# Two early loads of a convolution kernel moved from SyncE's queue to ScalarE's

## The chip, the cores and the metric

The kernel runs on one core of a Trainium2 chip. Times are microseconds on the device for one execution of the whole kernel; the lower the better. The time before is the median of three runs, 104.27 us (104.04 to 104.47).

## The reference

The reference is a 3x3 convolution with zero padding, stride 1 and no bias, followed by a 2x2 maximum pool. It takes 16 images of 64 channels and 64x64 pixels and gives 128 channels of 32x32, all in 32-bit floats:

```python
x_pad = np.pad(x, ((0, 0), (0, 0), (pad, pad), (pad, pad)))
conv[b, co] += weight[co, ci, kh, kw] * x_pad[b, ci, kh:kh+h, kw:kw+w]   # over ci, kh, kw
output[b, c, i, j] = np.max(conv[b, c, 2*i:2*i+2, 2*j:2*j+2])
```

## The kernel before

**Tiling.** Two images lie on the 128 partitions together, 64 channels each. A pair of images is cut into four chunks of 16 rows, and a chunk gives 8 pooled rows. There are 8 pairs, so 32 chunks, numbered 0 to 31 in the order in which they are worked. For each chunk and each of its two images (`l` = 0 or 1) TensorE makes products of 64 input channels against 128 output channels with up to 512 columns; the two images use the upper and the lower 64 rows of the array, so their products run in pairs. All arithmetic of TensorE is in bfloat16, its sums stand in eight PSUM banks.

**Two kinds of chunk.** Of the two rows that are pooled together, the kernel does not compute each with three row taps. It forms sums and differences of weights, and for some chunks of input rows too, so that a pair of rows needs fewer products. `SEQ` says which form a chunk takes. A `K` chunk (0, 2, 5, 9, 14, 18, 23, 27) needs five products, `PAa`, `PAb`, `PBa`, `PBb`, `PR`, and reads the input as bfloat16 rows, tile `kx`. A `W` chunk (all others, the first is 1) needs four products, `P2`, `P0`, `P3`, `P1`, and reads sums and differences of neighbouring rows, tiles `we`, `ws` and `wv`, which VectorE or GpSimd make from 32-bit input rows, tile `wx`.

**The order is written out by hand.** `ORDER` is a list of tokens; the loop at line 513 takes them one by one and emits the instructions of each. Every engine works its own instructions in the order in which the tokens name them, and waits on semaphores for what it needs. The letter after a colon names the engine of a step (`v` VectorE, `a` ScalarE, `g` GpSimd), or a digit names a PSUM bank. What is needed here:

- `LW` loads the weights into `wraw` (line 533). `LX.s` loads chunk `s` as 32-bit floats: a `W` chunk into `wx` (line 262), a `K` chunk into `kf` (line 268). `LX.0a` and `LX.0b` are the two halves of chunk 0. `LX.2` and `LX.4`, `LX.8`, `LX.6`, `LX.7`, `LX.10`, `LX.11` follow. All of these are issued by SyncE and stand in one DMA queue. Later K chunks are loaded by GpSimd with a cast on the way (`LK`, line 272). `ST` stores a finished chunk, mostly through SyncE's queue, the last ones partly through ScalarE's (line 495).
- `c.m` forms the weight block `m` (lines 191, 196), `T.m` transposes it on TensorE (line 229), `TV.m` copies it out of PSUM into `wt` (lines 240 to 244).
- `E.s`, `S.s`, `V.s` make the differences and sums of a W chunk (line 196, tiles `we`, `ws`, `wv`). With `CP.s` ScalarE first copies one row set into PSUM (line 287), and VectorE's `E` and `S` read it from there (line 291).
- `XO` and `XE` cast the odd or even rows of a K chunk from `kf` to `kx` (lines 191, 193).
- `EV` copies a finished sum out of PSUM (lines 420, 422), `SE` copies a sum from one bank into another as the start of the next one, a seed (line 436), `MX` takes the maximum over two rows (line 440), `OD` and `CM` that over two columns (lines 463, 472).

**The start.** The first tokens load the weights, then chunk 1 (`LX.1`), then the two halves of chunk 0, then chunk 3, and interleave this with forming the weights. On VectorE the steps are, in order: `c.GS`, `c.D0`, `c.GM`, `c.D2`, then `E.1`, `c.GP`, `V.1`, `TV.GP`, `XO.0a`. On ScalarE: `c.g1`, `c.g0`, `c.g2`, four `TV`, the seeds `SE.1.0` and `SE.1.1`, `XO.0b`, `XE.0a`, `CP.3`. On TensorE: eight products that only set the banks (line 500), the transposes, `P2.1` for both images, two more sets of transposes with one product of the tile `zeros` between them (line 430), then `P0.1`, `PAa.0` (upper half), `P3.1`, and from there on without end. The `zeros` product sets a PSUM bank that has held transposed weights to a defined state. The tile `zeros` is filled by VectorE with a memset, line 169.

**Semaphores of the queue.** SyncE's and ScalarE's loads and stores use eight semaphores in turn, so that the ninth is issued only once the first has landed.

Of the kernel before, what the change touches and what calls it, by code (L numbers as in the profile page):

```python
# [13 lines left out]
SEQ = "KWKWWKWWWKWWWWKWWWKWWWWKWWWKWWWW"  # L14
ADDED = ()
ORDER = """
LW c.g1:a c.GS:v c.D0:v LX.1 c.GM:v c.D2:v LX.0a c.g0:a T.G0:0 T.GM:1 T.G1:2 E.1:v c.g2:a T.D2:3
TV.GM:a TV.G0:a T.G2:4 TV.D2:a LX.0b LX.3 P2.1.0:5 P2.1.1:6 TV.G2:a c.GP:v SE.1.0:7 V.1:v T.D0:1
LX.2 SE.1.1:0 T.GP:3 LX.4 TV.GP:v XO.0b:a XO.0a:v P0.1.1 P0.1.0 PAa.0.0a:4 PAa.0.1a:3 S.1:g P3.1.0
P3.1.1 TV.D0:v LX.8 XE.0a:a CP.3:1 PAa.0.1b PAb.0.0a TV.G1:v E.3:v S.3:v EV.1.1 EV.1.0 XE.0b:a  # L20
PAa.0.0b PAb.0.1a MX.1.1 PBa.0.1a:2 PBa.0.0a:6 PAb.0.0b PAb.0.1b V.3:g PBb.0.0a PBb.0.1a LX.6 XE.2:a
# [62 lines left out]
def kernel(  # L84
# [7 lines left out]
    nc = tc.nc  # L92
    FP32 = mybir.dt.float32
    BF16 = mybir.dt.bfloat16
# [13 lines left out]
    const = ctx.enter_context(tc.tile_pool(name="const", bufs=1))  # L108
# [16 lines left out]
    def behind(inst, other):  # L125
        if other is not None:
            tc.add_manual_dep(inst.ins, other.ins.name, SYNC, reason="order")
# [7 lines left out]
    def rows_of(p, lo, hi):  # L135
        return x[2 * p : 2 * p + 2].rearrange("b c h w -> (b c) h w")[:, lo:hi, :]

    def chunk(s):

        p, q = place[s]  # L140
        same = any(place[t] == (p, q - 1) and SEQ[t] == SEQ[s] for t in range(N))
        lo = 2 * R * q + 1 if same else max(0, 2 * R * q - 1)
        return p, lo, min(H, 2 * R * (q + 1) + 1)

    def half(s):
        return 2 * R * place[s][1] + R + 1
# [18 lines left out]
    wq = const.tile([CO, 7, 2, 2, CI], BF16)  # L165
    wt = const.tile([128, 7 * K, CO], BF16)
    gsum = const.tile([CO, 3, CI], FP32)
    zeros = const.tile([128, 512], BF16)
    nc.vector.memset(zeros, 0.0)
    ident = const.tile([128, 128], BF16)  # L170
    make_identity(nc, ident)
    wv = wraw.rearrange("a (c k) -> a k c", k=K * K)

    def ring(t, k):
# [69 lines left out]
            nc.vector.tensor_copy(out=dst, in_=src)  # L244


    kf = {}
    done = {}
    AHEAD = {"W": 12, "K": 13}

    def paced(s, inst):

        for l in (0, 1):
            behind(inst, done.get((s - AHEAD[SEQ[s]], l)))
        if SEQ[s] == "K" and s < AHEAD["K"] and s not in kf:
            behind(inst, done["head"])

    def load(s, part, e):
        p, lo, hi = chunk(s)
        if SEQ[s] == "W":  # L260
            t = wx[p % NWX]
            paced(s, nc.sync.dma_start(out=t[:, lo + 1 : hi + 1, :], in_=rows_of(p, lo, hi)))
            return
        if s not in kf:
            kf[s] = const.tile([128, hi - lo, W], FP32, name=f"kf_{s}")
        a, b = {"": (lo, hi), "a": (lo, half(s)), "b": (half(s), hi)}[part]
        q = nc.scalar if e == "a" else nc.sync
        paced(s, q.dma_start(out=kf[s][:, a - lo : b - lo, :], in_=rows_of(p, a, b)))

    def load_cast(s):  # L270
# [242 lines left out]
    for token in ORDER.split():  # L513
        what, _, at = token.partition(":")
        name, *args = what.split(".")
        if name in PRODUCTS:
            s, l = int(args[0]), int(args[1][0])
# [20 lines left out]
        elif name == "LX":  # L538
            load(int(args[0].rstrip("ab")), args[0].lstrip("0123456789"), at)
        elif name == "LK":  # L540
            load_cast(int(args[0]))
        elif name == "CP":
            lift(int(args[0]), int(at))
        elif name in ("XO", "XE"):
            to_bf16(int(args[0].rstrip("ab")), args[0].lstrip("0123456789"), int(name == "XO"), at)
        elif name in ("KS", "S", "E", "V"):
            f = rs_cast if name == "S" and int(args[0]) in ADDED else None
            (f or {"KS": ks, "S": rs, "E": re, "V": rv}[name])(int(args[0]), at)
        elif name in ("Ve", "Vo"):
            rv_half(int(args[0]), at, int(name == "Vo"))  # L550
        elif name == "SA":
            rs_add(int(args[0]))
        elif name == "ST":
            l, part = (int(args[1][0]), args[1][1:]) if len(args) > 1 else (None, "")
            store(int(args[0]), l, part, at)
        else:
            s = int(args[0])
            l, part = (int(args[1][0]), args[1][1:]) if len(args) > 1 else (None, "")
            if name in ("SE", "SEv"):
                bank["B", s, l] = int(at)  # L560
                seed(s, l, name[2:])
                continue
            if name in ("OD", "CM", "RM"):
                {"OD": odd, "CM": colmax, "RM": pairmax}[name](s, l, part)
            else:
                {"EV": evac, "MX": rowmax}[name](s, l)
# [36 lines left out]
```

## Time and profile before

| What | Value |
|---|---|
| Median of three runs | 104.27 us |
| The profiled execution | 103.89 us |
| Its span, first to last instruction | 102.1 us |
| TensorE busy | 95.6 us, 94% |
| VectorE busy | 90.0 us, 88% |
| ScalarE busy | 89.6 us, 88% |
| GpSimd busy | 80.8 us, 79% |
| TensorE's granted clock | 1.0 of full speed throughout |
| Read from HBM, written | 17.07 MB, 8.39 MB |
| SyncE's queue (q1) | 12,624 packets, 22.16 MB |
| ScalarE's queue (q10) | 288 packets, 0.20 MB |

The profile is one execution, taken by the hardware profiler; its engines are PE (TensorE), PEld (TensorE's weight loads), DVE (VectorE), ACT (ScalarE), POOL (GpSimd) and SP (SyncE). An engine's name with a small q (SPq, ACTq) stands for the part that issues DMAs and waits on semaphores. In a row of the timeline stand the start, the duration, the engine, the line and the operation, what is written and read, the number of instructions merged, and in brackets how long the engine was idle before and what ended that. In a row of the DMA issues the last number is the time from issue to landing. The chain is followed back from the last instruction: at each step to what released it.

### The profile page before, as it was taken

Reading aid. Unit: us, or ns where it says so; the run is one execution under the profiler, and the core shown is the slowest. Engines: PE = TensorE matmul, PEld = TensorE weight load, DVE = VectorE, ACT = ScalarE, POOL = GpSimd, SP = SyncE. Lnnn points to the kernel's source line nnn. Section 1 sums busy time; section 2 is a strip of 40 time slices with the busy share of each in tenths; the row PEclk is TensorE's granted clock in tenths of the full one; section 3 lists DMA queues with packets and bytes.
Section 4 is the critical chain, followed back from the end, with each engine's and each line's share of the span. In section 5 each row is a group of like instructions: output and inputs, shape, how many; then the busy total and the mean of one; then the engine's idle time right before and its main releaser. Section 6 shows DMA issues by size and latency. Waiting matters only on the chain.

```text
span 102.1 us, 2481 instructions
## 1 busy us (share of the span) xinstructions
PE 95.6 (94%) x870; PEld 52.3 (51%) x870; DVE 90.0 (88%) x176; ACT 89.6 (88%) x200; POOL 80.8 (79%) x63
## 2 busy tenths in 40 slices
PE   6698999999999999999999999999999999999940
PEld 2155954555555567565555575555444446455310
DVE  1596999999989999999999999778989999998780
ACT  5597999888999999998899999999998988999930
POOL 5005998999599969999998999999971999999000
PEclk9999999999999999999999999999999999999999
DMA  2989999849940699999999971898769955302353
GB/s 42 343 235 414 418 419 335 181 113 356 263 122 0 165 219 324 250 322 328 255 404 350 377 287 28 251 251 219 282 213 311 340 179 180 128 32 74 132 182 103
DMA packets 13789, 24.07 MB, mean 236 GB/s; under 512 B 1104, under 2 KB 9680, under 8 KB 13776
## 3 DMA queue, kind: packets, MB, share of 16 engines
q1 hardware_dynamic: 12624, 22.16, 64.8%
q0 software_dynamic: 864, 1.56, 8.8%
q10 hardware_dynamic: 288, 0.20, 0.6%
q8 instruction: 7, 0.11, 0.4%
q14 instruction: 6, 0.05, 0.1%
HBM read 17.07 MB, written 8.39 MB: 249 GB/s over the span
## 4 chain that ended last, share of the span: by engine, by line
PE 84%; DVE 6%; DMA 3%; ACT 3%; issue 1%; ACTq 0%; DVEq 0%
PE acc L405 84%; DMA wraw<-in_weight_dram 3%; DVE wq L196 2%; ACT ev L420 1%; DVE wv L196 1%; ACT od L463 1%; DVE o L472 1%; DVE acc L440 1%; DVE we L196 1%; DVE gsum L196 0%; ACT acc L287 0%; ACT acc L436 0%; DVE wt L242 0%; DVE o L482 0%; ACTq L436 0%
## 5 line engine op out<-in xcount | busy, mean ns | idle before, releaser
L405 PEld LDWEIGHTS <-wt 64*128 64x128 bf16 x840 | 50.0, 94 | 40.6 <-issue 3.0
L405 PE MATMUL acc<-wv,wt 64*128 64x504 bf16 (+1 forms) x288 | 63.4, 377 | 0.5 <-DVE wt L242 0.5
L196 POOL TENSOR_TENSOR wv<-wx 128x1024 bf16<-128x1024 f32 x21 | 49.3, 2363 | 1.0 <-PE acc L405 0.4
L440 DVE TENSOR_TENSOR acc<-acc,ev 128x512 f32<-128x512 f32 x64 | 43.6, 692 | 2.7 <-ACT ev L420 1.4
L405 PE MATMUL acc<-kx,wt 64*128 64x504 bf16 (+6 forms) x216 | 38.6, 350 | 0.0
L405 PE MATMUL acc<-we,wt 64*128 64x512 bf16 (+1 forms) x144 | 36.9, 376 | 0.1
L405 PE MATMUL acc<-ws,wt 64*128 64x512 bf16 (+1 forms) x144 | 35.0, 377 | 0.2 <-DVE acc L440 0.2
L420 ACT ACTIVATE ev<-acc 128x512 f32<-128x512 f32 x48 | 28.8, 605 | 1.5 <-PE acc L405 1.2
L436 ACT COPY acc<-acc 128x512 f32<-128x512 f32 x48 | 28.2, 591 | 1.3 <-DVE o L472 0.4
L472 DVE TENSOR_TENSOR o<-acc,od 128x256 f32<-128x256 f32 x64 | 25.3, 414 | 2.1 <-ACT od L463 1.7
L463 ACT COPY od<-acc 128x256 f32<-128x256 f32 x64 | 23.0, 377 | 2.5 <-PE acc L405 1.2
L196 POOL TENSOR_TENSOR ws<-wx 128x512 bf16<-128x512 f32 x12 | 15.2, 1274 | 9.8 <-DVE kx L193 6.8
L196 POOL TENSOR_TENSOR we<-wx 128x512 bf16<-128x512 f32 x10 | 12.8, 1276 | 2.0 <-DVE ks L196 1.2
L405 PE MATMUL acc<-ks,wt 64*128 64x504 bf16 (+1 forms) x48 | 12.9, 376 | 0.0
L422 ACT COPY ev<-acc 128x512 f32<-128x512 f32 x16 | 9.3, 595 | 1.0 <-PE acc L405 0.8
L291 DVE TENSOR_TENSOR we<-acc,wx 128x512 bf16<-128x512 f32 x11 | 7.5, 683 | 1.2 <-ACT acc L287 1.1
L291 DVE TENSOR_TENSOR ws<-acc,wx 128x512 bf16<-128x512 f32 x11 | 7.5, 679 | 0.0
L287 ACT COPY acc<-wx 128x512 f32<-128x512 f32 x11 | 6.7, 606 | 0.6 <-DMA wx<-in_x_dram 0.6
L500 PE MATMUL acc<-const-bfloat16-1.0 128*128 128x512 bf16 x8 | 3.3, 585 | 0.8 <-PEq L584 0.8
L196 DVE TENSOR_TENSOR ks<-kx 128x512 bf16<-128x512 bf16 x8 | 4.0, 512 | 0.0
L196 DVE TENSOR_TENSOR wv<-wx 128x1024 bf16<-128x1024 f32 x3 | 3.7, 1217 | 0.0
L272 POOL DMA_DIRECT2D kx<-in_x_dram x6 | 3.5, 586 | 0.0
(28 smaller groups left out, 21.7 us busy)
## 6 DMA issues: line engine op xcount, KB each, us to landing
out_dram<-o SPq DMA_DIRECT2D x30, 256.0 KB, 3.5
wx<-in_x_dram SPq DMA_DIRECT2D x12, 512.0 KB, 7.1
wx<-in_x_dram SPq DMA_DIRECT2D x6, 544.0 KB, 5.1
wx<-in_x_dram SPq DMA_DIRECT2D x6, 480.0 KB, 7.7
kx<-in_x_dram POOLq DMA_DIRECT2D x3, 256.0 KB, 7.5
kf<-in_x_dram SPq DMA_DIRECT2D x1, 512.0 KB, 7.8
kx<-in_x_dram POOLq DMA_DIRECT2D x2, 240.0 KB, 7.8
wraw<-in_weight_dram SPq DMA_DIRECT2D x1, 288.0 KB, 3.0
```

Of the source, the lines that this page charges most:

```text
L196: inst = eng[e].tensor_tensor(out=out, in0=in0, in1=in1, op=op)
L272: paced(s, nc.gpsimd.dma_start(out=kx_of(p)[:, lo:hi, :], in_=rows_of(p, lo, hi)))
L287: nc.scalar.copy(out=acc[bank], in_=wrow(s, 0))
L291: nc.vector.tensor_tensor(out=t, in0=lifted[s], in1=wrow(s, 1), op=op)
L405: yield lambda kw=kw, o0=o0, o1=o1, c0=c0, c1=c1: nc.tensor.matmul(acc[t][:, i0:i1, o0:o1], wt[l * CI : l * CI + CI, K * BLOCKS[block] + T ...
L420: inst = nc.scalar.mul(t, acc[bank["A", s, l]], -1.0)
L422: inst = nc.scalar.copy(out=t, in_=acc[bank["A", s, l]])
L436: nc.scalar.copy(out=acc[b], in_=acc[bank["A", s, l]])
L440: nc.vector.tensor_tensor(out=t, in0=t, in1=ev[s, l], op=MAX)
L463: nc.scalar.copy(out=od[s, l][:, i0:i1], in_=acc[bank["B", s, l]][:, i0:i1, 1::2])
L472: done[s, l] = nc.vector.tensor_tensor(out=outs(s)[:, l, i0:i1], in0=acc[bank["B", s, l]][:, i0:i1, 0::2], in1=od[s, l][:, i0:i1], op=MAX,)
L500: nc.tensor.matmul(acc[n], ones[:, 0:128], ones, start=True, stop=True, skip_group_check=True)
```

## The change

Three things are changed. The loads of chunk 0, `LX.0a` and `LX.0b`, are marked `:a` and so issued by ScalarE. They stand right behind `LX.1` in the list, ahead of the weight steps. `LX.3` stands where it stood; SyncE, which no longer issues the two halves, issues it right after `LX.1`. And the tile `zeros` is no longer filled by VectorE's memset, but by ScalarE, which multiplies a constant tile of ones by 0.0; this is ScalarE's first computing instruction, and the load of its function table stands ahead of it. ScalarE's program now begins: table load, zeros, `LX.0a`, `LX.0b`, then `c.g1` as before. The helper `load` learns to choose the queue for W chunks too, which no token uses.

```diff
 ORDER = """
-LW c.g1:a c.GS:v c.D0:v LX.1 c.GM:v c.D2:v LX.0a c.g0:a T.G0:0 T.GM:1 T.G1:2 E.1:v c.g2:a T.D2:3
-TV.GM:a TV.G0:a T.G2:4 TV.D2:a LX.0b LX.3 P2.1.0:5 P2.1.1:6 TV.G2:a c.GP:v SE.1.0:7 V.1:v T.D0:1
+LW LX.1 LX.0a:a LX.0b:a c.g1:a c.GS:v c.D0:v c.GM:v c.D2:v c.g0:a T.G0:0 T.GM:1 T.G1:2 E.1:v c.g2:a
+T.D2:3 TV.GM:a TV.G0:a T.G2:4 TV.D2:a LX.3 P2.1.0:5 P2.1.1:6 TV.G2:a c.GP:v SE.1.0:7 V.1:v T.D0:1
...
-    zeros = const.tile([128, 512], BF16)
-    nc.vector.memset(zeros, 0.0)
     ident = const.tile([128, 128], BF16)
     make_identity(nc, ident)
+    zeros = const.tile([128, 512], BF16)
+    nc.scalar.mul(zeros, nc.const_aps.tensor(1.0, [128, 512], BF16), 0.0)
...
+    queue = {"s": nc.sync, "a": nc.scalar}
...
             t = wx[p % NWX]
-            paced(s, nc.sync.dma_start(out=t[:, lo + 1 : hi + 1, :], in_=rows_of(p, lo, hi)))
+            q = queue[e or "s"]
+            paced(s, q.dma_start(out=t[:, lo + 1 : hi + 1, :], in_=rows_of(p, lo, hi)))
...
-        q = nc.scalar if e == "a" else nc.sync
+        q = queue[e or "s"]
         paced(s, q.dma_start(out=kf[s][:, a - lo : b - lo, :], in_=rows_of(p, a, b)))
```

## The prediction

> **What bounds the kernel now.** I read the page's busy shares first, then the chain that ended last, then the first 15 us engine by engine in order of time, then the DMA issues with their landing times. The page and the chain:
>
> ```profile
> span 102.1 us, 2481 instructions
> PE 95.6 (94%) x870; PEld 52.3 (51%) x870; DVE 90.0 (88%) x176; ACT 89.6 (88%) x200; POOL 80.8 (79%) x63
> ```
> ```profile
> 0.74 3.02 DMA wraw<-in_weight_dram
> ...
> 4.29 1.58 DVE wq L196 x3
> 5.87 0.60 DVE we L196
> ...
> 7.00 1.07 DVE wv L196
> ...
> 8.50 36.38 PE acc L405 x350
> ...
> 47.48 48.56 PE acc L405 x442
> ```
>
> The first number of a chain row is its start, the second its length. From 8.50 us to 96 us the chain is TensorE's, with one break of 2.6 us around 45. So the kernel is a head of 8.50 us, about 88 us of products that wait for almost nothing, and a tail. What delays the first dense product delays the end by as much; an operand that comes earlier behind that point gains only what TensorE stands still there. The change lies in the head, so the head is what I price. Its order of time on VectorE, ScalarE and TensorE:
>
> ```profile
> 0.87 0.27 DVE L169 MEMSET zeros<- 128x256 uint32 x1 [0.87 <-PEq L584]
> ...
> 3.79 0.51 DVE L196 TENSOR_TENSOR gsum<-wraw 128x192 f32<-128x192 f32 x1 [2.65 <-DMA wraw<-in_weight_dram]
> ...
> 5.79 0.68 DVE L196 TENSOR_TENSOR we<-wx 128x512 bf16<-128x512 f32 x1
> ...
> 6.92 1.22 DVE L196 TENSOR_TENSOR wv<-wx 128x1024 bf16<-128x1024 f32 x1
> 8.13 0.36 DVE L242 TENSOR_SCALAR wt<-acc 128x384 bf16<-128x384 bf16 x1
> ...
> 10.31 0.69 DVE L291 TENSOR_TENSOR we<-acc,wx 128x512 bf16<-128x512 f32 x1 [1.08 <-ACT acc L287]
> ```
> ```profile
> 0.74 1.28 ACT L191 ACT_TABLE_LOAD   x1 [0.74 <-PEq L584]
> ...
> 7.37 1.08 ACT L436 COPY acc<-acc 128x512 f32<-128x512 f32 x2
> 8.36 0.77 ACT L191 CAST kx<-kf 128x256 bf16<-128x256 f32 x2
> 9.68 0.59 ACT L287 COPY acc<-wx 128x512 f32<-128x512 f32 x1 [0.56 <-DMA wx<-in_x_dram]
> ```
> ```profile
> 6.53 0.82 PE L405 MATMUL acc<-we,wt 64*128 64x512 bf16 x6
> ...
> 8.50 0.82 PE L405 MATMUL acc<-wv,wt 64*128 64x512 bf16 x6 [0.49 <-DVE wt L242]
> ```
>
> VectorE's `we` at 5.79 (E.1) is the first thing made from the first W chunk, LX.1. It ends at 6.47; P2.1's products start at 6.53 and end at 7.35; ScalarE's two seeds start at 7.37 and end at 8.45; the products of 8.50 (P0.1) go into the bank that the second seed has read. VectorE's own path, E.1, then `wv` (V.1), then the L242 copy that ends at 8.49, meets the same point. Both paths go through E.1, and neither has 0.1 us to spare: **whatever E.1 waits, TensorE's dense part starts that much later.** So when does LX.1 land?
>
> ```profile
> 0.74 0.37 SPq L533 DMA_DIRECT2D wraw<-in_weight_dram  x1
> 1.17 0.42 SPq L262 DMA_DIRECT2D wx<-in_x_dram  x1
> 1.64 0.90 SPq L268 DMA_DIRECT2D kf<-in_x_dram  x2
> 2.58 0.43 SPq L262 DMA_DIRECT2D wx<-in_x_dram  x1
> ```
> ```profile
> wx<-in_x_dram SPq DMA_DIRECT2D x1, 544.0 KB, 4.4
> wraw<-in_weight_dram SPq DMA_DIRECT2D x1, 288.0 KB, 3.0
> kf<-in_x_dram SPq DMA_DIRECT2D x1, 288.0 KB, 5.8
> kf<-in_x_dram SPq DMA_DIRECT2D x1, 256.0 KB, 6.2
> ```
> ```profile
> wx<-in_x_dram SPq DMA_DIRECT2D x1, 512.0 KB, 7.0
> ```
>
> The last column is issue to landing. One queue serves them in order: weights 0.74+3.0 = 3.74, LX.1 1.17+4.4 = 5.57, LX.0a 1.64+5.8 = 7.4, LX.0b (second issue of that row, 2.1) +6.2 = 8.3, LX.3 2.58+7.0 = 9.6. LX.1 has 5.79-5.57 = 0.22 us of slack, no more.
>
> **The change part by part.**
> *The zeros tile.* VectorE loses a memset of 0.27 us in a stretch where it idles 2.65 us for the weights: nothing. ScalarE gains one 128x512 instruction; the nearest row is its copy of that size:
>
> ```profile
> L436 ACT COPY acc<-acc 128x512 f32<-128x512 f32 x48 | 28.2, 591 | 1.3 <-DVE o L472 0.4
> ```
>
> So 0.59 us behind the table load, which ends at 2.02: 2.02 to 2.61, and the first cast waits for the weights (3.74) anyway. Nothing; if that cover were gone it would be 0.59 us. The zeros are read only behind the products of 6.53. The table load stands at 0.74 in either kernel.
>
> *SyncE loses two issues.* 0.90 us and two gaps: LX.3 is issued at about 1.64 instead of 2.58, everything behind it 0.94 us earlier. Issues are not the limit, the data are (next fence), so this shifts the order, not the sum of the bytes. Later loads wait for a semaphore that a load of eight before has used; LX.11 now waits for LX.3 instead of LX.0b. In its row it was in the queue for 11.4 us:
>
> ```profile
> wx<-in_x_dram SPq DMA_DIRECT2D x1, 480.0 KB, 11.4
> ```
>
> A later issue by about 1 us is hidden by that.
>
> *ScalarE's queue gains two issues*, of some 0.42 us each by SyncE's rows. When? Only at the end of the kernel before does ScalarE issue loads or stores:
>
> ```profile
> 98.94 0.27 ACT L463 COPY od<-acc 128x128 f32<-128x128 f32 x1 [0.82 <-DVE o L482]
> 98.94 0.96 ACTq L495 DMA_DIRECT2D out_dram<-o  x2
> ```
>
> The first store stands behind that copy in ScalarE's program and is issued as the copy begins, not as it ends: the issuing part does not wait for the computing part. Nothing in the new program makes the two loads wait, so I take it that they are issued at about 0.8 and 1.25 us, while the table load runs, beside the weights (0.74) and LX.1 (1.17). The other end is an issue behind table load and zeros, at 2.6 and 3.0; then ScalarE is free at 3.5, still ahead of 3.74. I choose the early end because the row shows an issue beside running work. The Trainium skill says the same on the page "Perfetto Trace Analysis", section on the DVE / Act engine instruction: the sequencer decodes on while an instruction sits in the execution FIFO; no run here shows it for a table load.
>
> *What the second queue does to the first.* Beside each other, two queues are seen later, when GpSimd's loads (q0) run beside SyncE's (q1), here between 16 and 18.5 us:
>
> ```profile
> q0 software_dynamic: 131, 0.26, 54.7%
> q1 hardware_dynamic: 144, 0.48, 51.4%
> ```
>
> 131 packets against 144: the 16 engines take about one from each in turn, whatever came first. And they have nothing to spare (last two columns: busy share of the DMA engines, GB/s):
>
> ```profile
> 1.50:2.00 0.50, 0.50 (x2) 0.15 (x1) 0.00 (x0) 0.50 (x1) 0.39 (x2) 1.00 1.00 124
> ...
> 2.50:3.00 0.50, 0.50 (x3) 0.22 (x2) 0.00 (x0) 0.00 (x0) 0.00 (x0) 1.00 0.94 371
> ...
> 5.50:6.00 0.50, 0.48 (x8) 0.31 (x8) 0.50 (x2) 0.26 (x2) 0.00 (x0) 1.00 0.67 123
> ```
>
> LX.0a and LX.0b have 128 packets each, one to a partition, as the weights and LX.1 have. In turn, LX.0a goes beside the weights and LX.0b beside LX.1. In the kernel before, LX.1 had landed when 832 KB were through; now up to 1376 KB must be through. Before, these four loads had all landed at 8.3: the upper end for LX.1. The lower end is 5.57, no sharing. Between them: the weights and LX.0a are 576 KB instead of 288, and 288 KB more at 371 GB/s are 0.8 us; I take 0.6, since the weights' issue leads, so weights at about 4.35, and VectorE reaches E.1 at 5.79+0.6 = 6.4. LX.1 and LX.0b are 800 KB more; at 371 GB/s from about 4.1 that gives 6.3, at the slow pace of the middle stretch the 8.3 above. **I take 7.3, the middle.** E.1 then starts 7.3-5.79 = 1.5 us late, and P0.1 with it.
>
> The Trainium skill, page "DMA: Bandwidth & Descriptors", section "Queues, rings and completion order", has the engines go round the queues packet by packet, and means by a packet some 9 to 17 descriptors, not one. By that rule LX.1 would come behind the weights and LX.0a but ahead of LX.0b, when 1120 KB are through, which by LX.0a's row is 7.4: the sum would be 0.1 us higher, where one-by-one turns give 7.3. The trace of the two queues above fits the turns but not the size.
>
> *What comes earlier.* The halves no longer stand in LX.1's wake, so LX.0a and LX.0b land by about 7.3 too, ahead of ScalarE's casts at 8.36, which are now 1.5 us later: nothing late next there. LX.3 stands behind 1888 KB as before, so about 9.6 or a little earlier; its reader at 9.68, now at 11.2, no longer waits its 0.56 us, and VectorE's 1.08 us behind it shrink. TensorE can use of that between nothing and 0.56 us; I take 0.3. Past 16 us everything is shifted alike.
>
> Sum: +1.5 (E.1 on LX.1) -0.3 (LX.3 no longer awaited) = +1.2 us. On the profiled execution's 103.89 us (span 102.1 and 1.8 around it) that is 105.1. The median of the runs, 104.27, lies 0.38 above it: **105.5 us**. With the ends: 8.3 and nothing regained is +2.5 (106.8); no sharing and all regained is -0.56 (103.7).
>
> **The rivals.**
> (a) Main case, above: issue at 0.8, LX.1 at 7.3: 105.5.
> (b) ScalarE's issues come only behind table load and zeros, at 2.6. The first weights' packets move about 1 us behind their issue (the row of 1.50), so the halves begin near 3.6. With half of LX.1 then left, some 144 KB of LX.0a slip in; at 371 to 123 GB/s that is 0.4 to 1.2 us, so LX.1 at 6.4 and E.1 0.6 late. But LX.0b now shares with LX.3 and ends near 10 instead of 8.3; ScalarE's cast of it, at 8.36+0.6, waits 1 us and delays what stands behind it on ScalarE, where 0.56 us were idle anyway: +0.6+0.4 = +1.0, 105.3. For it: the table load is ScalarE's own work. Against: the rows of 98.94.
> (c) Faster: the second queue does not delay LX.1, because the turns favour the queue that began or the halves fill the start, when only 124 GB/s move. Then E.1 starts at 5.79 and LX.3 lands up to 0.94 us earlier, which removes ScalarE's 0.56 us: 104.27-0.56 = 103.7. It decides from the point where LX.1 lands by 5.79. Against: 0.22 us of slack with a full DMA share from 2.5 on.
> (d) No change that can be measured: what LX.1 loses (up to 0.5 us) LX.3 gives back: 104.3. The same page of the Trainium skill, in "Issuing engines are not separate DMA queues", says that issuing from several engines saves only issue time and the transfers interleave all the same. Worked out from the rows, only SyncE's 0.94 us of earlier issue would stay, on a queue that is full for 10 us: nothing.
>
> **How the numbers follow.** (a) 0.53, (b) 0.19, (c) 0.15, (d) 0.13. Half a per cent, 0.5 us, is about what a measurement of this kernel can tell from no change; (a) and (b) lie above it, (c) below, so faster 0.15, same 0.13, slower 0.72. The range must take in the upper end of LX.1's landing less a little regained, 106.6, and reach to (d) and most of (c): 103.8 to 106.6. The likeliest case's own range is 104.7 to 106.6.
>
> **What would show it.** ScalarE's queue: first issue near 0.8 or near 2.6 tells (a) from (b). E.1's row (`we<-wx` on VectorE, 5.79 before): start near 7.3 and a wait put down to the wx load. First cast of `wq`: near 4.4 instead of 3.79. First dense `wv` products: near 10.0 instead of 8.50. ScalarE's copy of the third W load without its 0.56 us of idling. The prediction is wrong if LX.1 lands before 5.8, if the weights and LX.1 land late but TensorE's dense part makes it up, or if the end moves by other than the start of the dense part.

## The result, and the profile after

The changed kernel takes 107.40 us (median of four runs, 106.49 to 107.55) where the kernel before takes 104.16 (four runs): the ratio is 1.029, with a 95% interval of 1.0243 to 1.0336. It is slower by 3.2 us. The forecast was slower by 1.2, and 107.40 lies above its range. In the ratios, here and below, executions more than 1.5% above the fastest of their kernel are left out. The profiled execution of the changed kernel took 107.48 us, its span is 105.7 against 102.1.

The page of the changed kernel and its chain (start, length, what):

```profile
span 105.7 us, 2481 instructions
...
PE 98.1 (93%) x870; PEld 53.4 (51%) x870; DVE 89.7 (85%) x175; ACT 90.7 (86%) x201; POOL 80.8 (76%) x63
```
```profile
1.17 6.09 DMA wx<-in_x_dram
...
7.29 0.70 DVE we L196
...
8.03 1.46 PE acc L407 x6
...
9.93 0.44 PE acc L432
...
11.01 37.45 PE acc L407 x350
...
51.05 48.56 PE acc L407 x442
```

In the kernel before, the head's chain began with the weights; here it begins with LX.1. E.1 starts at 7.29 instead of 5.79, 1.50 us late. The first dense products, P0.1, start at 11.01 instead of 8.50, 2.51 late. The second long piece of the chain starts at 51.05 instead of 47.48, 3.57 late, and that is the whole difference of the spans, 3.6. So the loss has three parts: **1.50 us up to E.1, 1.01 more between E.1 and P0.1, 1.06 more within the first dense piece**, whose 350 products take 37.45 us instead of 36.38. Those 1.06 are a net figure. The thirty products of chunk 0 behind P3.1 start 4.05 us late (before, then changed), and TensorE makes up about 0.5 us of that by 23 us:

```profile
10.12 1.87 PE L405 MATMUL acc<-kx,wt 64*128 64x256 bf16 x30
```
```profile
14.17 1.79 PE L407 MATMUL acc<-kx,wt 64*128 64x256 bf16 x30
```

The first part is the one that was forecast. E.1's row, ScalarE's timeline, and the DMA issues of the first 4 us (the last column is issue to landing):

```profile
7.29 0.69 DVE L196 TENSOR_TENSOR we<-wx 128x512 bf16<-128x512 f32 x1 [1.02 <-DMA wx<-in_x_dram]
```
```profile
0.74 1.28 ACT L171 ACT_TABLE_LOAD   x1 [0.74 <-PEq L586]
0.80 0.87 ACTq L270 DMA_DIRECT2D kf<-in_x_dram  x2
2.03 0.63 ACT L171 ACTIVATE zeros<-const-bfloat16-1.0 128x512 bf16<-128x512 bf16 x1
4.18 1.75 ACT L191 CAST wq<-wraw 128x256 bf16<-128x256 f32 x3 [1.52 <-DMA wraw<-in_weight_dram]
```
```profile
wx<-in_x_dram SPq DMA_DIRECT2D x1, 544.0 KB, 6.1
...
wraw<-in_weight_dram SPq DMA_DIRECT2D x1, 288.0 KB, 3.4
kf<-in_x_dram ACTq DMA_DIRECT2D x1, 288.0 KB, 3.8
kf<-in_x_dram ACTq DMA_DIRECT2D x1, 256.0 KB, 6.8
```

The two loads are issued from 0.80 us on, while the table load still runs and before the zeros are made: the program's order did not hold them back. The weights land at 0.74+3.4 = 4.1 instead of 3.7, LX.0a at 0.80+3.8 = 4.6 instead of 7.4, LX.1 at 1.17+6.1 = 7.3 instead of 5.6, LX.0b at 8.0. LX.0a went beside the weights, and LX.0b beside LX.1. The 1.50 us hold for this pair of executions: in the three profiles with the changed loads E.1 starts at 7.29, 7.53 (`warm`) and 7.34 (`warm2`), in the three with the loads of the kernel before at 5.79, 5.62 (`zeros_only`) and 6.58 (`before_fill`).

The other two parts have another cause. TensorE's rows, and the windows around them (PEclk, the granted clock, is the third number from the end; 1.00 is full speed):

```profile
8.03 1.46 PE L407 MATMUL acc<-we,wt 64*128 64x512 bf16 x6 [1.20 <-DVE we L196]
...
11.01 1.47 PE L407 MATMUL acc<-wv,wt 64*128 64x512 bf16 x6 [0.34 <-ACT acc L438]
```
```profile
7.00:7.50 0.50, 0.00 (x0) 0.00 (x0) 0.21 (x1) 0.50 (x3) 0.00 (x0) 0.93 1.03 414
7.50:8.00 0.50, 0.00 (x0) 0.00 (x0) 0.50 (x2) 0.30 (x1) 0.00 (x0) 0.50 1.04 426
...
14.00:14.50 0.50, 0.50 (x9) 0.33 (x7) 0.00 (x0) 0.38 (x1) 0.50 (x1) 0.74 1.02 408
```

While TensorE waits 1.20 us for E.1, its granted clock falls to 0.50. The mean of 0.93 puts the fall at 7.43, that of 0.74 the return at 14.26. In these 6.83 us it works at half speed: the six products of P2.1 take 1.46 us instead of 0.82, those of P0.1 1.47 instead of 0.82. P0.1 itself now waits for ScalarE's second seed (L438), which stood behind the slowed product of the `zeros` tile, 0.63 us instead of 0.38. Three of the four executions have a mean granted clock of 0.955 or 0.956 and took 107.31 to 107.55; the fourth, with 0.997, took 106.49. A mean tells little of the first microseconds: the time before a trace's first record of the clock counts as full speed, though TensorE works at half speed there (the eight products at the start of the changed kernel take 3.47 us, five products of the same size in `warm` 1.25).

### The profile page after: what moved, and what is told of

It is laid out like the page before. It is cut to its first block, busy times and chain, and to the rows that moved or that the text cites. A ratio compares the mean times of both kernels' runs of the same rounds, so it can differ in the third digit from the quotient of the medians.

```text
span 105.7 us, 2481 instructions
## 1 busy us (share of the span) xinstructions
PE 98.1 (93%) x870; PEld 53.4 (51%) x870; DVE 89.7 (85%) x175; ACT 90.7 (86%) x201; POOL 80.8 (76%) x63
## 4 chain that ended last, share of the span: by engine, by line
PE 84%; DMA 6%; ACT 3%; DVE 2%; issue 1%; SPq 0%; ACTq 0%; DVEq 0%
PE acc L407 84%; DMA wx<-in_x_dram 6%; ACT ev L422 1%; ACT acc L438 1%; ACT od L465 1%; DVE o L474 1%; DVE acc L442 1%; DVE we L196 1%; ACT acc L289 0%; PE acc L432 0%; PE acc L229 0%; SPq L535 0%; DVE o L484 0%; ACTq L438 0%; DVEq L442 0%
## 5 line engine op out<-in xcount | busy, mean ns | idle before, releaser
L407 PEld LDWEIGHTS <-wt 64*128 64x128 bf16 x840 | 50.8, 95 | 42.1 <-issue 5.8
L407 PE MATMUL acc<-wv,wt 64*128 64x504 bf16 (+1 forms) x288 | 64.5, 387 | 0.3 <-ACT acc L438 0.3
L407 PE MATMUL acc<-we,wt 64*128 64x512 bf16 (+1 forms) x144 | 37.4, 386 | 1.2 <-DVE we L196 1.2
L438 ACT COPY acc<-acc 128x512 f32<-128x512 f32 x48 | 28.2, 590 | 3.2 <-PE acc L407 2.1
L196 DVE TENSOR_TENSOR gsum<-wraw 128x192 f32<-128x192 f32 x1 | 0.5, 504 | 4.2 <-DMA wraw<-in_weight_dram 4.2
```

The lines of the kernel that those rows point to most:

```text
L196: inst = eng[e].tensor_tensor(out=out, in0=in0, in1=in1, op=op)
L407: yield lambda kw=kw, o0=o0, o1=o1, c0=c0, c1=c1: nc.tensor.matmul(acc[t][:, i0:i1, o0:o1], wt[l * CI : l * CI + CI, K * BLOCKS[block] + T ...
L438: nc.scalar.copy(out=acc[b], in_=acc[bank["A", s, l]])
```

## The experiments

Times are medians, and each ratio is to the kernel before, run in the same session.

**warm: TensorE kept busy in its pauses.** This tells the lateness of LX.1 from the clock.

```diff
+c.D2:v c.g0:a F.4 T.G0:0 ...  TV.D2:a LX.3 F.5 P2.1.0:5     # F.n: n products of ones into bank 7
```

> The changed kernel with nine products of ones more on TensorE, into a bank that is free then: four while it waits for the first weight block, five while it waits for E.1. Theory (LX.1 late by 1.5 us, and TensorE's idling of 1.2 us before 8.03 us then halves its granted clock, which is worth the other 2 us): E.1 still starts near 7.3, the first dense wv products near 10.0 instead of 11.0, no window at clock 0.5 before 14 us, time 105.7. Rival (the 2 us come from operands that are late in the dense part, the clock is only a symptom): granted clock near 1.0 but the time stays near 107.4.

Measured: 105.49 us, ratio 1.0103 (1.0067 to 1.0139). VectorE's E.1, TensorE's P2.1 and P0.1, and the core's mean clock:

```profile
7.53 0.69 DVE L196 TENSOR_TENSOR we<-wx 128x512 bf16<-128x512 f32 x1 [1.14 <-DMA wx<-in_x_dram]
```
```profile
8.27 0.82 PE L407 MATMUL acc<-we,wt 64*128 64x512 bf16 x6 [0.23 <-DVE we L196]
...
10.24 0.82 PE L407 MATMUL acc<-wv,wt 64*128 64x512 bf16 x6 [0.49 <-DVE wt L242]
```
```profile
core 0: 103.6 us, clock 0.998
```

E.1 is at least as late as in the changed kernel (7.53 against 7.29), but the products run at full speed (0.82 us for six), and E.1's 1.74 us of lateness arrive at P0.1 as 1.74 and at the end of the span as 1.5. Nine products that compute nothing take the loss from 2.9% to 1.0%. The rival falls.

**warm2: only two products more, in the second pause.**

```diff
+TV.D2:a LX.3 F.2 P2.1.0:5
```

> The changed kernel with only two products of ones more on TensorE, in its second pause. Theory: TensorE's busy share in the stretch before 7.5 us rises from about 0.50 to 0.62, near the 0.67 at which the kernel before keeps its clock, so the clock stays at 1.0 in most executions: 105.5. Rival (it takes a filled pause): the clock is halved as before, 107.4.

Measured: 106.01 us, ratio 1.0166 (1.0119 to 1.0213). Between the two expectations. The profiled execution was of another kind: its P2.1 took 1.47 us, yet its P0.1 ran at full speed, 0.82. TensorE had never left the slow start there; its first record of full speed comes at 9.97 us, where the changed kernel has it at 4.02. The mean clocks of the four executions, 0.989 to 1.0, leave no room for a later stretch of 6.83 us at half speed, and all four took 105.72 to 106.36, so the rival's 107.4 falls. Whether two products are enough when the clock has come up early, no profile shows.

**zeros_only: the kernel before with the zeros on ScalarE.**

```diff
-    nc.vector.memset(zeros, 0.0)
+    nc.scalar.mul(zeros, nc.const_aps.tensor(1.0, [128, 512], BF16), 0.0)
```

> The kernel before with only the zeros tile moved to ScalarE. Theory: no change, 104.2 within 0.3, E.1 at 5.8. Rival (ScalarE's longer start delays its first cast): first cast after 3.9, time above 104.6.

Measured: 104.18 us, ratio 0.9987 (0.9948 to 1.0026), E.1 at 5.62, the first cast at 3.62. As expected: this part of the change costs nothing.

**one_half: only LX.0a on ScalarE's queue.**

```diff
-LW LX.1 LX.0a:a LX.0b:a c.g1:a
+LW LX.1 LX.0a:a LX.0b c.g1:a
```

> The changed kernel with only LX.0a on ScalarE's queue; LX.0b goes back to SyncE's, behind LX.1. Theory (the engines take from both queues in turn, so what is ahead of LX.1 are the bytes served beside it): weights still land near 4.15, LX.1 then runs nearly alone and lands at 6.2 to 6.5, E.1 0.4 to 0.7 us late, TensorE's clock stays at 1.0, time 104.6 to 105.0. Rival (a second queue costs LX.1 the same whatever it carries): LX.1 near 7.3, time 107.4.

Measured: 105.55 us, ratio 1.0081 (1.0034 to 1.0128), between 104.49 and 106.89. Its DMA issues:

```profile
wx<-in_x_dram SPq DMA_DIRECT2D x1, 544.0 KB, 5.4
...
wraw<-in_weight_dram SPq DMA_DIRECT2D x1, 288.0 KB, 3.8
```

LX.1 lands at 1.17+5.4 = 6.6, a little above the 6.2 to 6.5 of the theory and well ahead of 7.3, so the rival falls. But the expectation missed the clock: in the profiled execution the weights landed at 4.5, TensorE paused 1.48 us for them, and its clock was halved from 7.66 to 11.08.

**one_queue: no second queue, both halves ahead of LX.1.**

```diff
-LW LX.1 LX.0a:a LX.0b:a c.g1:a
+LW LX.0a LX.0b LX.1 c.g1:a
```

> All four loads on SyncE's queue, but both halves ahead of LX.1. Theory (only the bytes ahead of LX.1 count, not the queue): LX.1 lands at 7.3 to 8.3, E.1 with it, TensorE idles over 1.2 us and its clock is halved, time 107.4 to 108.6. Rival (two queues side by side cost the engines time of their own): LX.1 clearly ahead of 7.2, time below 106.5.

Measured: 109.33 us, ratio 1.0462 (1.0375 to 1.0549).

```profile
9.50 0.69 DVE L196 TENSOR_TENSOR we<-wx 128x512 bf16<-128x512 f32 x1 [3.92 <-DMA wx<-in_x_dram]
```

E.1 waits until 9.50, 1.2 us past the upper end that the theory gave, TensorE stands still for 4.09 us, and its clock is halved from 7.65 to 14.47. That bytes ahead of LX.1 delay it is confirmed; their price is not a fixed one. The 16 engines finished LX.0b's shares between 4.5 and 7.2 us here, and between 7.4 and 8.0 in the changed kernel; why they drift apart so far was not settled.

**late and held: the halves issued later.** In `late` they stand behind ScalarE's first cast, in `held` behind one small instruction that waits for the zeros.

```diff
-LW LX.1 LX.0a:a LX.0b:a c.g1:a
+LW LX.1 c.g1:a LX.0a:a LX.0b:a                       # late
```
```diff
+    nc.scalar.mul(zeros[:, 0:128], ident, 0.0)       # held, behind the zeros
```

> The changed kernel with both halves issued by ScalarE only behind its first cast, which waits for the weights. Theory (turns between the queues from the moment the second one has packets): issues at 3.8 and 4.3, weights at 3.7, LX.1 before 5.9, E.1 at 5.8 to 6.0 and TensorE's clock at 1.0; but the 256 packets of the halves now go in turn with LX.1's rest, LX.3 and LX.2, so LX.0b lands at 10 to 11 instead of 8.3 and ScalarE's cast of it holds TensorE up by 1 to 2 us: 105.2 to 106.2. Rival (the early issue was not the cause of E.1's lateness): E.1 stays near 7.3.

> The changed kernel with one more small instruction on ScalarE behind the zeros, which has to wait for the zeros themselves, so that the two loads are issued only near 2.7 us, the prediction's rival (b). Theory (both queues' loads are turned into packets one after the other in the order of issue, so what SyncE has issued before 2.7 us goes ahead): LX.1 lands by 5.9 and E.1 starts at 5.8 to 6.0; the first packet of LX.0a comes over 2 us behind its issue, LX.0b lands at 10 to 11.5, and TensorE waits for chunk 0: 105.5 to 107. Rival (the prediction's turns from 1 us behind the issue): LX.1 lands near 6.4, LX.0b near 10, 105.3.

Measured: `late` 108.31 us, ratio 1.0414 (1.0377 to 1.0452); `held` 108.21 us, ratio 1.0359 (1.0301 to 1.0417). `late` is clearly slower than the changed kernel, `held` by its median (the two intervals overlap). ScalarE's issues and its cast of LX.0b, first in `late`, then in `held`:

```profile
3.83 1.15 ACTq L270 DMA_DIRECT2D kf<-in_x_dram  x2
...
13.13 0.76 ACT L191 CAST kx<-kf 128x256 bf16<-128x256 f32 x2 [4.25 <-DMA kf<-in_x_dram]
```
```profile
2.78 1.37 ACTq L271 DMA_DIRECT2D kf<-in_x_dram  x2
...
13.34 0.77 ACT L192 CAST kx<-kf 128x256 bf16<-128x256 f32 x2 [3.32 <-DMA kf<-in_x_dram]
```

And the queues that moved anything in `late` between 3.8 and 7.8 us:

```profile
DMA packets 317, 1.18 MB, mean 296 GB/s; under 512 B 32, under 2 KB 32, under 8 KB 317
## 3 DMA queue, kind: packets, MB, share of 16 engines
q1 hardware_dynamic: 317, 1.18, 97.5%
```

Only SyncE's queue. The first packet of ScalarE's queue (q10) starts at 7.90, 4.1 us behind its issue; in `held` it is 6.88, also 4.1 us behind; in the changed kernel 2.74, 1.9 us behind (1.5 and 1.8 in `warm` and `warm2`); a load of SyncE into an empty queue needs 1.0 (0.74 to 1.75). SyncE had issued six loads ahead of ScalarE's in `late`, five in `held`, one in the changed kernel. So the turns between the queues do not begin at the issue. Loads issued earlier on the other queue go ahead first, as if both queues passed one common point in the order of issue. This fits all three runs, but that point itself is not seen in a trace. In `late` E.1 comes at 6.20, where SyncE's load is hardly disturbed, so that rival falls; the halves land at 11.2 and 13.1 instead of 7.4 and 8.3, and TensorE waits for chunk 0. In `held` E.1 comes at 6.72, later than the theory had it, and the halves land at 11.4 and 13.3. No packet of ScalarE's queue had moved before LX.1 landed there, at 6.70, so turns between the queues are not the reason; `before_fill`, with the loads of the kernel before, has 6.58. The sizes of both expectations were too small, and the rival's 1 us from issue to packet is refuted.

**late_fill and before_fill: three products of ones in the first pause.**

```diff
+c.g0:a F.3 T.G0:0
```

> As the late issue, with three products of ones more on TensorE while it waits for the first weight block. Theory: in the head TensorE is busy enough without them, so the time is that of the late issue within 0.4 us. Rival (the halved clock takes part there too): more than 1 us faster than the late issue.

> The kernel before with the same three products more. Theory: its clock stays at 1.0 in nearly all executions, so the median stays at 104.2 to 104.4, and the few executions above 106 us are gone, if they are executions with a halved clock. Rival: the median falls by over 0.5 us, the clock costs the kernel before something in most executions.

Measured: `late_fill` 109.19 us, ratio 1.0493 (1.0446 to 1.054), 0.9 us slower than `late`; `before_fill` 104.35 us, ratio 1.0041 (1.0017 to 1.0066), five runs from 104.15 to 104.57. The clock does fall in `late`, but later, from 11.15 to 14.56, when TensorE waits for chunk 0, and in `late_fill` from 14.22 to 17.63; the added products, at 4.07, stand too early to help there. Why `late_fill` lost 0.9 us (the intervals just overlap): in its profile ScalarE's second issue took 1.52 us instead of 0.73 and held its casts up; whether that is its rule or this one execution is open. In `before_fill` nothing is gained, so its rival falls; five executions are too few to tell whether the rare ones above 106 us are gone.

**split_w: the weights in two halves of 64 partitions, one on each queue** (with the zeros on ScalarE).

```diff
-            nc.sync.dma_start(out=wraw, in_=...)
+            nc.sync.dma_start(out=wraw[0:64], in_=flat[0:64])
+            nc.scalar.dma_start(out=wraw[64:128], in_=flat[64:128])
```

> The kernel before with the zeros tile on ScalarE and the weights loaded in two halves of 64 partitions, one on each queue; the other loads as before. Theory (the second queue hurts only by the bytes it puts ahead; these are the same bytes): weights land at 3.5 to 3.8, E.1 at 5.5 to 5.8, time 103.9 to 104.4. Rival (a second queue in use costs the first one time of its own): weights after 4.0 and time above 104.8.

Measured: 105.36 us, ratio 1.015 (1.0133 to 1.0168). The theory was wrong here, and the rival's two numbers came true, but not quite for its reason:

```profile
4.38 0.51 DVE L196 TENSOR_TENSOR gsum<-wraw 128x192 f32<-128x192 f32 x1 [4.38 <-DMA wraw<-in_weight_dram]
```

The weights are complete at 4.3 instead of 3.7, though no byte more is loaded. SyncE's half landed at 3.46, ScalarE's at 4.28. ScalarE's half, issued 0.06 us behind SyncE's, sent its first packet at 2.68, as in the changed kernel. So the first queue's half was not held back; the second's came late. And the later weights are only a part of the 1.5%. In the profile E.1 starts at 6.39, 0.60 us late, but P0.1 at 10.28, 1.78 late, because the clock comes up only at 9.40 and P2.1 runs at half speed:

```profile
7.39 1.46 PE L405 MATMUL acc<-we,wt 64*128 64x512 bf16 x6
```

Whether it came up late in the other three executions too is not on record.

**order_only: all on SyncE's queue, LX.3 ahead of the halves.**

```diff
-LW LX.1 LX.0a:a LX.0b:a c.g1:a ... LX.3
+LW LX.1 LX.3 LX.0a LX.0b c.g1:a ...
```

> All loads on SyncE's queue, in the order weights, LX.1, LX.3, LX.0a, LX.0b, so the same going over from the first W chunk to the next, without a second queue. Theory (the order counts, not the queue): E.1 at 5.8 and the clock at 1.0, LX.3 lands near 8, the halves at 9.0 and 9.6 instead of 7.4 and 8.3, which costs TensorE 0.2 to 0.8 us in front of chunk 0: 104.4 to 105.0. Rival (LX.3 ahead of the halves is a gain in itself): 103.7 or less.

Measured: 104.17 us, ratio 0.9995 (0.9967 to 1.0022). Neither expectation. The loads landed about as the theory had it (LX.3 at 7.7, the halves at 8.9 and 9.5; E.1 at 6.13), but LX.3 1.9 us earlier and the halves 1.2 to 1.4 us later together neither gain nor cost. In this order, without the second queue, the change would have been neutral. No version beat the kernel before by more than its interval.

**When the clock falls.** TensorE's busy time in the 3.41 us up to the moment at which its clock fell, or in the same stretch where it stayed; the kernels are, in order, before (stayed), late_fill (stayed), late (stayed), one_half (fell), changed (fell):

```profile
3.65:7.06 3.41, 2.31 (x23) 1.16 (x21) 3.27 (x7) 3.03 (x7) 0.00 (x0) 1.00 0.94 241
```
```profile
3.98:7.39 3.41, 1.88 (x19) 1.04 (x17) 3.10 (x7) 2.01 (x5) 0.00 (x0) 1.00 0.90 269
```
```profile
4.32:7.74 3.42, 1.83 (x23) 1.19 (x23) 3.12 (x7) 2.83 (x7) 0.00 (x0) 1.00 1.00 313
```
```profile
4.25:7.66 3.41, 1.75 (x20) 1.13 (x21) 3.08 (x6) 2.83 (x6) 0.00 (x0) 1.00 0.95 322
```
```profile
4.02:7.43 3.41, 1.59 (x16) 0.94 (x16) 2.23 (x5) 3.01 (x7) 0.00 (x0) 1.00 0.98 315
```

2.31, 1.88 and 1.83 us of 3.41 kept the clock, 1.75 and 1.59 lost it. By this profile's modelled busy times the edge in these heads lies between 51% and 54%, on these few executions. Busy time alone is not the whole rule: at the end of the changed kernel the clock falls at 103.01 behind a stretch with 2.04 of 3.42 us busy, 60%, in which six products ran one after another (1.40 us instead of 0.82). What exactly is counted is not seen here.

## Why the prediction was wrong

**What was right.** That the head sets the end and E.1 sets the head; that ScalarE issues at 0.8 and 1.25 us beside its table load (0.80 and 1.21); that LX.0a would go beside the weights and LX.0b beside LX.1; LX.1 at 7.3 and E.1 1.5 us late (7.3 and 1.50); weights at about 4.35 (4.1); the zeros at nothing (`zeros_only` 0.9987); about 0.3 us regained behind P0.1 (in `warm` 1.74 us at P0.1 are 1.5 at the end of the span); "Past 16 us everything is shifted alike" (the shift is 3.57 from 23 us to the end). That 7.3, chosen as the middle between 6.3 and 8.3, came out to a tenth is in part luck, and so is how close `warm`, the predicted case without what the prediction forgot, comes to the predicted 105.5 with its 105.49; against its own kernel before it is slower by 1.07 us, where 1.2 was forecast. The 0.22 us of slack were read from one execution; with the same loads LX.1 landed a whole microsecond later in `before_fill`, at 6.56.

**What failed** is the step "E.1 then starts 7.3-5.79 = 1.5 us late, and P0.1 with it". P0.1 came 2.5 us late, and the dense part behind it ran its first 3.25 us, 11.01 to 14.26, at half speed. The prediction priced TensorE's pause as waiting only. It should have asked what the pause does to the clock: in the kernel before TensorE is busy for 2.31 us of the 3.41 ahead of 7.06, in the changed kernel for 1.59 of the 3.41 ahead of the fall. The term that is missing from the sum is the clock's: 1.01 us before P0.1 and 4.05-2.51 = 1.54 behind it, 2.55 in the profile, of which TensorE makes up more than the 0.3 forecast: 1.50+2.55-0.48 = 3.57. By medians, each against its own kernel before, the changed kernel loses 3.24 us and `warm` 1.07, so the clock is worth 2.2. The prediction's own last sign of being wrong came true with it: the end moved by 3.57, the start of the dense part by 2.51.

The Trainium skill has this gate on the page "TensorE: Matmul & The Clock Gate", in "Part 1: The HAM clock gate": half speed by default, judged over free-running windows of 3413 ns. The trace agrees on the two speeds and on the window: the slow stretch of 6.83 us is two of them. It does not agree that it takes an idle window, or a gap of over 3.4 us as the section on HAM oscillation has it: here two pauses of 1.18 and 1.20 us were enough, with TensorE busy for 1.59 us of the 3.41.

**The rivals.** (b) fell twice: the issue was not held back, and where it was (`held`), the first packet came 4.1 us behind it, not 1. (c) asked for LX.1 by 5.79; it landed at 7.3. (d) had LX.3 give back what LX.1 loses, up to 0.5 us; LX.1 lost more, and in `warm` only about 0.3 came back. The two rules for the turns that the prediction compared, 7.3 and 7.4, lie too close for these runs to tell apart. The Trainium skill's sentence on the page "DMA: Bandwidth & Descriptors", in "Issuing engines are not separate DMA queues", that a second issuing engine saves only issue time holds for the interleaving, but leaves out a cost: `split_w` moved no byte more, and its weights were complete at 4.28 us instead of 3.76.

## What to carry to other kernels

In this kernel a load moved to a second queue did not run beside the first for nothing: its packets took turns with those of the load that the critical path waits for, and it took longer to start the more loads the other queue had already been given (1.9 us behind one, 4.1 behind five or six). Before pricing a longer wait of TensorE in a head, add up its busy time in the 3.41 us ahead: in these heads 51% and less halved the clock, 54% and more kept it, and in this kernel that cost more than the wait itself. Nine products that compute nothing, placed in the pauses, brought this back, though not the wait.

## What the runs showed of the hardware that was not expected

- ScalarE's queue is slow to start even when it is empty: 1.5 to 1.9 us from issue to first packet behind one load of SyncE's (0.80 to 2.74 in the changed kernel), 4.1 us behind five or six, against 1.0 for SyncE's first load.
- The issues themselves get longer then, and hold up ScalarE's own work: two took 0.87 us in the changed kernel, 1.15 in `late`, 1.37 in `held`.
- The clock fell on two pauses of 1.2 us in the changed kernel and one of 1.5 in `one_half`, at a modelled busy share of 47 and 51%, and came back only after two stretches of 3.41 us and one.
- The slow start does not end at the same time: the first record of full speed stands between 3.65 and 5.60 us in ten profiles, and at 8.82, 9.40 and 9.97 in `held`, `split_w` and `warm2`. In these three P2.1 ran at half speed (1.46 or 1.47 us).
- Between about 4 and 7 us the DMA engines moved less than their later 420 GB/s in every kernel: the slowest half microsecond had 246 GB/s in the changed kernel, 123 in the kernel before and 115 in `split_w`. It is not the small packets alone, since a 4352-byte load is slowed as well, and it was not settled what it is.
